# Layer 1's end: the output weights in the pool opened first, the residual rows at the head of the pool that follows

## The chip, the cores and the metric

The kernel runs on one core of a Trainium2 chip. The metric is the time of one execution on the device in microseconds; a change is judged by the medians of repeated runs of the kernel before and after it. The profile shows one execution of the kernel before, taken by the hardware profiler: the engines TensorE (PE; its weight loads PEld), VectorE (DVE), ScalarE (ACT), GpSimd (POOL) and SyncE (SP), whose queue issues the DMAs spoken of here.

## What is computed

An encoder of two layers over 2048 positions of 1024 features. Each layer is a mixer between a modulation and a normalisation with a residual:

```python
for layer in range(DEPTH):
    mod = cond @ ada_w[layer] + ada_b[layer]
    shift, scale, gate = jnp.split(mod, 3, axis=-1)
    h = x * (1.0 + scale[:, None, :]) + shift[:, None, :]
    y = even_mixer(...) if layer % 2 == 0 else odd_mixer(...)
    x = layer_norm(DEEPNORM_ALPHA * x + gate[:, None, :] * y, ln_g[layer], ln_b[layer])
```

The change lies in layer 1, whose mixer is a gated linear recurrence, run forwards and backwards over the positions:

```python
xr, g = jnp.split(h @ w_in, 2, axis=-1)
xr = centred_depthwise_conv(xr, conv_w, conv_b)
y = (rg_lru(xr, w_a[0], b_a[0], w_x[0], b_x[0], lam[0], reverse=False)
     + rg_lru(xr, w_a[1], b_a[1], w_x[1], b_x[1], lam[1], reverse=True))
return (y * jax.nn.silu(g)) @ w_out
```

## The kernel before

The positions are worked on in four tiles of C = 512 (t = 0 to 3); features lie in KD = 8 blocks of 128, called k or g. A matrix product keeps its operands as a high and a low part (hi, lo; made by `split`: ScalarE copies hi at L154, VectorE subtracts at L155) and needs three products on TensorE (`mm3`, L158 to L160): hi by hi, hi by lo, lo by hi.

Layer 1 sweeps the tiles forwards. The forward recurrence can be finished in that sweep; the backward one runs from the last position to the first, so for the tiles 0 to 2 the sweep stores what the backward one will need: for even blocks the coefficients, the inputs, the forward result and the gate (a_d, b_d, f_d, g_d), for odd blocks two arrays that need only one number per row of correction (u_d, v_d). For the last tile, t = 3, both directions are done within the sweep: `front` makes the recurrence of four blocks at a time, `back` multiplies by the gate (L1034), stores two columns to y_d (L1040), and splits the result into the operands y3 of the output product. The four blocks k = 4 to 7 come last, by `back(NT - 1, 1, f1, G1)`.

What follows the sweep:

- The output product of the last tile: `part_out` adds one block k for four groups b of 128 positions, 12 products for each half n of the 1024 output features, into the eight accumulators ps3. All 16 weight tiles (two halves by eight blocks, 512 KB each, wo_d in memory) stay in SBUF to the end: those of k = 0 to 3 in the ring of the sweep's weights (`hl`), those of k = 4 to 7 by `resident` (L1079), as tiles that are made once.
- `load_y(t)`: for t = 2, 1, 0, the operands of the output product. For an even k it loads at, bt, ft, gt (L1106, two buffers each), scans backwards on VectorE (L1113), copies one column and adds on GpSimd (L1116, L1117), multiplies by the gate on VectorE (L1118) and splits; for an odd k it loads ut and vt, corrects on VectorE (L1127) and splits. For t = 2, two columns more come from y_d (L1130).
- The residual rows z of a tile (L1151 in the kernel before, L1144 after), four of [128, 1024], from a ring of six; the sum z = ALPHA z + product on VectorE (L1166, L1179 and L1195 in the kernel before); then the normalisation: BN_STATS (L614) and an aggregate (L616) on VectorE, 1/sqrt on GpSimd (L150, L151), two steps over 1024 columns on VectorE (L623, L624), a store (L625).

Two things set the order. A scheduler orders each engine's instructions when the kernel is built, starting from the order of the text; each engine, and SyncE's queue of DMAs, then runs its own list strictly in order. And pools of SBUF are stacked from two sides: a pool that is opened after another on its side was closed takes over its memory, and each tile in it waits until whatever lay there is no longer used. Here `oq` (left) takes over from the sweep's pool `front` (closed by `sf.close()`), which held the convolution's tiles X, xc, xhi, xlo; `op` (right) takes over from `rnn` (closed by `se.close()`), which held hg, ra, T, ii, G and sg, in use until the end of `back`.

Of the kernel before, what the change touches and what calls it, by code (L numbers as in the profile page):

```python
# [7 lines left out]
F32 = mybir.dt.float32  # L8
# [10 lines left out]
KD = D // 128  # L19
C = 512  # L20
NT = S // C
# [32 lines left out]
def kernel(  # L54
# [39 lines left out]
    def pool(stack, name, side=None, bufs=1, space=None):  # L94
        kw = {} if space is None else {"space": space}
        if side is not None:
            kw["side"] = side
        return stack.enter_context(tc.tile_pool(name=name, bufs=bufs, reuse_waits="tile", **kw))
# [54 lines left out]
    def split(hi, lo, src):  # L153
        act(out=hi, in_=src, func=AF.Copy)  # L154
        tt(out=lo, in0=src, in1=hi.bitcast(F32), op=ALU.subtract)  # L155

    def mm3(ps, ahi, alo, bhi, blo, first, last):
        nc.tensor.matmul(ps, lhsT=ahi, rhs=bhi, start=first, stop=False)  # L158
        nc.tensor.matmul(ps, lhsT=ahi, rhs=blo, start=False, stop=False)  # L159
        nc.tensor.matmul(ps, lhsT=alo, rhs=bhi, start=False, stop=last)  # L160

    def bank(p, tag, shape=(128, C)):
        t = p.tile(list(shape), F32, tag=tag, name=tag)
        return t
# [353 lines left out]
    def act_pair():  # L518
        hi = cp.tile([128, 2, C], F32R, tag="act", bufs=12, name="ahi")
        lo = cp.tile([128, 2, C], F32R, tag="act", bufs=12, name="alo")  # L520
        return hi, lo
# [62 lines left out]
    def banks():  # L584
        if turn is None:
            return [bank(pj, "pj") for _ in range(4)]
        r = []
        for _ in range(4):
            r.append(bank(*((pja, "pja"), (px, "px"), (pjb, "pjb"))[turn[0] % 6 // 2]))
            turn[0] += 1  # L590
        return r
# [478 lines left out]
    def part_out(ps, hl, k):  # L1070
        for b in range(4):
            sl = slice(b * 128, b * 128 + 128)
            mm3(ps[b], y3[0][k][:, sl], y3[1][k][:, sl], hl[:, 0], hl[:, 1], k == 0, k == KD - 1)

    wo = [[None] * KD, [None] * KD]

    def resident(p, n, k):
        w = p.tile([128, 2, C], F32R, name=f"wo{n}_{k}")
        nc.sync.dma_start(out=w.bitcast(F32), in_=wo_d[n * KD + k])  # L1079
        wo[n][k] = w  # L1080

    ps3 = [banks(), [bank(pj, "pj")] + [bank(pm, "pm") for _ in range(3)]]
# [3 lines left out]
            part_out(ps3[n], wo[n][k], k)  # L1086

    oq = pool(ctx, "outq", left)
    for k in (4, 5):
        for n in range(2):  # L1090
            resident(oq, n, k)
    back(NT - 1, 1, f1, G1)
# [6 lines left out]
    def load_y(t):  # L1099
        y = ([], [])  # L1100
        n = C if t < NT - 2 else C - 2
        c0 = t * C

        def fetch(tag, src, k):
            p = oq.tile([128, C], F32, tag=tag, bufs=2, name=tag)
            load(out=p[:, 0:n], in_=src[:, k, c0:c0 + n])  # L1106
            return p

        for k in range(KD):
            if k % 2 == 0:  # L1110
                at, bt, ft, gt = (fetch(tag, src, k) for tag, src in (("at", a_d), ("bt", b_d), ("ft", f_d), ("gt", g_d)))
                h = bt[:, 0:n]
                nc.vector.tensor_tensor_scan(out=h[:, ::-1], data0=at[:, 0:n][:, ::-1], data1=h[:, ::-1],  # L1113
                                             initial=carry_b[:, t + 1, k:k + 1], op0=ALU.mult, op1=ALU.add)
                if t > 0:
                    nc.gpsimd.tensor_copy(carry_b[:, t, k:k + 1], bt[:, 0:1])  # L1116
                nc.gpsimd.tensor_tensor(out=ft[:, 0:n], in0=ft[:, 0:n], in1=h, op=ALU.add)  # L1117
                stt(out=ft[:, 0:n], in0=ft[:, 0:n], scalar=0.5, in1=gt[:, 0:n], op0=ALU.mult, op1=ALU.mult)  # L1118
                if t == NT - 2 or k < 4:
                    hi, lo = act_pair()  # L1120
                else:
                    hi, lo = (op.tile([128, 2, C], F32R, tag="act2", bufs=8, name=nm) for nm in ("ahi", "alo"))
            else:
                ft, vt = (fetch(tag, src, k // 2) for tag, src in (("ut", u_d), ("vt", v_d)))
                for u, q0, q1 in ((t, 0, C - 2), (t + 1, C - 2, C)):
                    if u < NT - 1:
                        stt(out=ft[:, q0:q1], in0=vt[:, q0:q1], scalar=cr[:, u, k // 2:k // 2 + 1],  # L1127
                            in1=ft[:, q0:q1], op0=ALU.mult, op1=ALU.add)
            if n < C:
                load(out=ft[:, n:C], in_=y_d[:, k, :])  # L1130
            split(hi[:, k % 2], lo[:, k % 2], ft)
            y[0].append(hi[:, k % 2])
            y[1].append(lo[:, k % 2])
        return y

    y2 = load_y(NT - 2)
    se.close()


    op = pool(ctx, "outp", right)  # L1140
    for k in (6, 7):
        for n in range(2):
            resident(op, n, k)
    for k in range(4, KD):  # L1144
        for n in range(2):
            part_out(ps3[n], wo[n][k], k)

    def residual_tile(t, b):
        r = t * C + b * 128
# [4 lines left out]
    zt = [residual_tile(NT - 1, b) for b in range(4)]  # L1154
    g_bc = op.tile([128, D], F32, name="g_bc1")
    b_bc = op.tile([128, D], F32, name="b_bc1")
    load(out=g_bc, in_=ln_g[1:2, :].broadcast_to([128, D]))
    load(out=b_bc, in_=ln_b[1:2, :].broadcast_to([128, D]))
    def finish(t, b, z):
# [67 lines left out]
```

## Time and profile before

| what | value |
|---|---|
| median of 3 runs (lowest, highest) | 1569.88 us (1568.82, 1575.3) |
| the profiled execution | 1567.64 us |
| its span, first to last instruction | 1565.9 us |
| busy PE, DVE, ACT, POOL | 1480.2, 1186.2, 784.1, 404.7 us |
| mean granted TensorE clock | 0.983 |

The profiled execution lies 2.2 us under the median of the runs. All moments in the text are microseconds from the span's start. A PE record of a product of 512 columns lasts 0.39 us and the next starts about 0.23 us after it, since products are pipelined; rates are therefore taken from start to start. The same holds for VectorE, where a record of 0.68 us is followed by the next after 0.60. An idle time in square brackets stands with what ended it.

### The profile page before, as it was taken

Reading aid. Unit: us, or ns where it says so; the run is one execution under the profiler, and the core shown is the slowest. Engines: PE = TensorE matmul, PEld = TensorE weight load, DVE = VectorE, ACT = ScalarE, POOL = GpSimd, SP = SyncE. Lnnn points to the kernel's source line nnn. Section 1 sums busy time; section 2 is a strip of 40 time slices with the busy share of each in tenths; the row PEclk is TensorE's granted clock in tenths of the full one; section 3 lists DMA queues with packets and bytes.
Section 4 is the critical chain, followed back from the end, with each engine's and each line's share of the span. In section 5 each row is a group of like instructions: output and inputs, shape, how many; then the busy total and the mean of one; then the engine's idle time right before and its main releaser. Section 6 shows DMA issues by size and latency. Waiting matters only on the chain. (4 is left out here: it accounts for less than half of the span.)

```text
span 1565.9 us, 22099 instructions
## 1 busy us (share of the span) xinstructions
PE 1480.2 (95%) x7096; PEld 1185.7 (76%) x7096; DVE 1186.2 (76%) x2180; ACT 784.1 (50%) x1470; POOL 404.7 (26%) x488
## 2 busy tenths in 40 slices
PE   7999999989999999999999999999999999869997
PEld 3887777657878777788887787787788788747886
DVE  4599889755859568967767775987987697788985
ACT  4677767542523332343244228499498496841100
POOL 1023233211005000300120231634644432133221
PEclk9999999999999999999999999999999999989999
DMA  9357766839788989988785699788777766369751
GB/s 348 130 170 219 224 196 189 265 120 304 243 281 298 257 255 298 314 276 262 260 296 177 195 263 275 231 259 283 224 249 271 236 226 220 111 204 340 257 193 54
DMA packets 209211, 370.91 MB, mean 237 GB/s; under 512 B 56616, under 2 KB 103620, under 8 KB 209096
## 3 DMA queue, kind: packets, MB, share of 16 engines
q1 hardware_dynamic: 202344, 354.53, 70.2%
q0 software_dynamic: 6752, 14.98, 3.7%
q8 instruction: 56, 0.92, 0.2%
q14 instruction: 59, 0.48, 0.1%
HBM read 261.96 MB, written 85.97 MB: 222 GB/s over the span
## 5 line engine op out<-in xcount | busy, mean ns | idle before, releaser
L154 ACT ACTIVATE hl<-raw 128x512 fp32r<-128x512 f32 x192 | 119.1, 628 | 227.3 <-DMA raw<-in_ev_w_in_dram 142.2
L159 PE MATMUL pj<-alo,hl 128*128 128x512 f32 x512 | 200.7, 392 | 0.0
L158 PE MATMUL pj<-ahi,hl 128*128 128x512 f32 x512 | 199.5, 392 | 1.1 <-DVE gz L753 1.1
L160 PE MATMUL pj<-ahi,hl 128*128 128x512 f32 x512 | 199.6, 391 | 0.0
L155 DVE TENSOR_TENSOR hl<-raw,hl 128x512 fp32r<-128x512 f32 x192 | 131.8, 695 | 71.5 <-ACT hl L154 70.7
L150 POOL TENSOR_SCALAR rstd<-mv 128x1 f32<-128x1 f32 x32 | 31.0, 970 | 416.5 <-DVE mv L616 305.8
L158 PEld LDWEIGHTS pj<-ahi,hl 128*128 128x128 f32 x512 | 96.5, 189 | 22.0 <-DVE gz L753 1.5
L159 PEld LDWEIGHTS pj<-alo,hl 128*128 128x128 f32 x512 | 96.6, 189 | 20.3
L160 PEld LDWEIGHTS pj<-ahi,hl 128*128 128x128 f32 x512 | 96.4, 188 | 20.2
L465 POOL DMA_DIRECT2D P<-T x112 | 62.6, 566 | 177.7 <-DVE nm L430 78.0
L158 PE MATMUL pj<-wqh,hhi 128*128 128x256 f32 (+1 forms) x256 | 88.5, 350 | 2.5 <-ACT hhi L154 1.7
L430 DVE CUSTOM_DVE_ANT_0 P<-psc,mask,nsink 128x384 f32<-128x384 f32 (+1 forms) x128 | 73.8, 593 | 22.1 <-PE psc L429 22.0
L154 ACT ACTIVATE phl<-praw 128x512 fp32r<-128x512 f32 x56 | 35.4, 631 | 105.9 <-DMA praw<-in_od_w_in_dram 51.1
L159 PE MATMUL pj<-wql,hhi 128*128 128x256 f32 (+1 forms) x256 | 88.0, 344 | 0.0
L160 PE MATMUL pj<-wqh,hlo 128*128 128x512 f32 (+1 forms) x256 | 85.7, 347 | 1.5 <-DVE hlo L155 1.5
L977 DVE SCALAR_TENSOR_TENSOR ii<-ii,xc 128x1024 f32<-128x1024 f32 (+2 forms) x32 | 40.6, 1269 | 57.6 <-ACT ii L971 57.6
L433 ACT ACTIVATE P<-P,nm 128x384 f32<-128x384 f32 (+1 forms) x128 | 76.4, 601 | 10.3 <-DVE nm L430 10.1
L777 POOL TENSOR_TENSOR alo<-hm,ahi 128x512 fp32r<-128x512 f32 x32 | 48.5, 1524 | 118.5 <-DVE hm L776 99.7
L947 DVE SCALAR_TENSOR_TENSOR xc<-X,vcol,xc 128x512 f32<-128x512 f32 (+2 forms) x96 | 75.2, 818 | 0.3
L158 PE MATMUL pm<-xhi,hg 128*128 128x512 f32 (+3 forms) x160 | 55.6, 361 | 14.1 <-ACT xhi L154 6.5
L155 DVE TENSOR_TENSOR phl<-praw,phl 128x512 fp32r<-128x512 f32 x56 | 39.1, 698 | 35.2 <-ACT phl L154 33.0
L775 ACT ACTIVATE ahi<-hm,shift,scale 128x512 fp32r<-128x512 f32 x32 | 25.2, 812 | 74.1 <-DVE hm L774 66.8
(304 smaller groups left out, 4320.1 us busy)
## 6 DMA issues: line engine op xcount, KB each, us to landing
hl<-w_d SPq DMA_DIRECT2D x128, 512.0 KB, 4.7
raw<-in_ev_w_in_dram SPq DMA_DIRECT2D x128, 256.0 KB, 4.0
w_d<-phl SPq DMA_DIRECT2D x40, 512.0 KB, 4.6
aw<-in_ada_w_dram SPq DMA_DIRECT2D x32, 512.0 KB, 6.9
hg<-w_d SPq DMA_DIRECT2D x32, 512.0 KB, 5.4
P<-T SPq DMA_DIRECT2D x104, 96.0 KB, 4.8
P<-T POOLq DMA_DIRECT2D x104, 96.0 KB, 4.2
aw<-in_ada_w_dram SPq DMA_DIRECT2D x8, 1024.0 KB, 7.7
```

What stands on the lines that cost most here:

```text
L150: nc.gpsimd.tensor_scalar(out=dst, in0=src, scalar1=mul, scalar2=EPS, op0=ALU.mult, op1=ALU.add)
L154: act(out=hi, in_=src, func=AF.Copy)
L155: tt(out=lo, in0=src, in1=hi.bitcast(F32), op=ALU.subtract)
L158: nc.tensor.matmul(ps, lhsT=ahi, rhs=bhi, start=first, stop=False)
L159: nc.tensor.matmul(ps, lhsT=ahi, rhs=blo, start=False, stop=False)
L160: nc.tensor.matmul(ps, lhsT=alo, rhs=bhi, start=False, stop=last)
L430: nc.vector.tensor_tensor_reduce(out=p[:, g, 0:W], in0=ps[:, 0:W], in1=mask[:, m0:m0 + W], scale=-0.125, scalar=nsink[:, h:h + 1], op0=ALU ...
L433: act(out=p[:, g, 0:W], in_=p[:, g, 0:W], func=AF.Exp, scale=-1.0, bias=nm[:, h:h + 1], accum_out=rs[:, h:h + 1])
L465: dma.dma_start(out=pv[32 * r:32 * r + 32, 0:nb, i], in_=T[32 * i:32 * i + 32, 0:nk].rearrange("p (j r) m -> p r j m", r=4)[:, r])
L777: nc.gpsimd.tensor_tensor(out=lo[:, j], in0=h, in1=hi[:, j].bitcast(F32), op=ALU.subtract)
L947: stt(out=xc[:, w], in0=xt[:, j0 + j:j0 + j + W], scalar=vcol1[:, 8 * j + g:8 * j + g + 1], in1=xc[:, w], op0=ALU.mult, op1=ALU.add)
L977: stt(out=ii[i][:, :, w], in0=ii[i][:, :, w], scalar=1.0, in1=xc[:, None, w].to_broadcast([128, 2, W]), op0=ALU.add, op1=ALU.mult)
```

## The change

```diff
     oq = pool(ctx, "outq", left)
-    for k in (4, 5):
+    for k in range(4, KD):
         for n in range(2):
             resident(oq, n, k)
     back(NT - 1, 1, f1, G1)
...
         def fetch(tag, src, k):
-            p = oq.tile([128, C], F32, tag=tag, bufs=2, name=tag)
+            p = op.tile([128, C], F32, tag=tag, bufs=2, name=tag)
             load(out=p[:, 0:n], in_=src[:, k, c0:c0 + n])
             return p
...
-    y2 = load_y(NT - 2)
     se.close()
     op = pool(ctx, "outp", right)
-    for k in (6, 7):
-        for n in range(2):
-            resident(op, n, k)
-    for k in range(4, KD):
-        for n in range(2):
-            part_out(ps3[n], wo[n][k], k)
...
     zt = [residual_tile(NT - 1, b) for b in range(4)]
     g_bc = op.tile([128, D], F32, name="g_bc1")
     b_bc = op.tile([128, D], F32, name="b_bc1")
+    y2 = load_y(NT - 2)
+    for k in range(4, KD):
+        for n in range(2):
+            part_out(ps3[n], wo[n][k], k)
+
     load(out=g_bc, in_=ln_g[1:2, :].broadcast_to([128, D]))
```

The weights of k = 6 and 7 move from `op` to `oq`, beside those of 4 and 5. The twelve buffers of `load_y` (24 KB of each partition) move from `oq` to `op`, so from the memory of the convolution's tiles to that of the recurrence's, behind the six residual rows and the two rows of the normalisation. In the text, the loads of the last tile's residual rows now come ahead of `load_y(2)`, and the products of k = 4 to 7 behind it.

On SyncE's queue, after the weights of k = 5 (a row is one DMA, target and source; wo_d_86 and wo_d_94 are the two halves of k = 6, wo_d_87 and wo_d_95 of k = 7):

```order
 L1079 DMA wo_5_13369<-wo_d_93 128x1024
+L1079 DMA wo_6_13371<-wo_d_86 128x1024
+L1079 DMA wo_6_13373<-wo_d_94 128x1024
+L1079 DMA wo_7_13375<-wo_d_87 128x1024
+L1079 DMA wo_7_13377<-wo_d_95 128x1024
+L1040 DMA y_d<-T 128x2 x2
+L1144 DMA z<-x_d 128x1024 x4
 L1106 DMA at<-a_d 128x510
 L1106 DMA bt<-b_d 128x510
```

The weights of k = 6, 7, the last two stores to y_d and the four residual rows now stand ahead of the first load of tile 2. Before, the same weights stood behind most of that tile's loads:

```order
 L1106 DMA gt<-g_d 128x510
-L1079 DMA wo_6_13501<-wo_d_86 128x1024
 L1106 DMA ut<-u_d 128x510
 L1130 DMA ut<-y_d 128x2
-L1079 DMA wo_6_13503<-wo_d_94 128x1024
```

On VectorE, from the last scan of the sweep on (L1113 is the scan, which these rows call by its other name; cr is the correction of the odd blocks, alo<-T the split of the last tile's k = 6 and 7), before:

```order
L1010 COPY carry_b<-T 128x1
L1113 SCALAR_TENSOR_TENSOR bt<-at,carry_b,bt 128x510
L1010 COPY carry_b<-T 128x1
L1034 SCALAR_TENSOR_TENSOR T<-T,G 128x514
L1094 COPY cr<-carry_b 128x4
```

and after, from the last of these splits on:

```order
L155 TENSOR_TENSOR alo<-T,ahi 128x512
L1164 SCALAR_TENSOR_TENSOR z<-z,pj 128x512 x2
L614 BN_STATS st_13625<-z 128x6
L1164 SCALAR_TENSOR_TENSOR z<-z,pj 128x512
L614 BN_STATS st_13636<-z 128x6
L1113 SCALAR_TENSOR_TENSOR bt<-at,carry_b,bt 128x510
L1164 SCALAR_TENSOR_TENSOR z<-z,pj 128x512 x2
L1164 SCALAR_TENSOR_TENSOR z<-z,pm 128x512 x2
L1127 SCALAR_TENSOR_TENSOR ut<-vt,cr,ut 128x510
L1164 SCALAR_TENSOR_TENSOR z<-z,pm 128x512
L614 BN_STATS st_13625<-z 128x6
L1118 SCALAR_TENSOR_TENSOR ft<-ft,gt 128x510
```

Tile 2's first scan moves from ahead of the last tile's gate product to behind three of the last tile's residual sums, and its later steps are mixed with that tile's normalisation.

On TensorE the products of tile 2 begin, in the kernel after, with the high parts of k = 0 for both halves (hl_13248 is the weight of half 0, hl_13304 of half 1; ahi_13431 and alo_13432 hold k = 0 and 1), before the low part is used:

```order
L158 MATMUL pj_13677<-hl_13248,ahi_13431 128x512
L159 MATMUL pj_13677<-hl_13248,ahi_13431 128x512
...
L158 MATMUL pm_13784<-hl_13304,ahi_13431 128x512
L159 MATMUL pm_13784<-hl_13304,ahi_13431 128x512
L160 MATMUL pj_13677<-hl_13248,alo_13432 128x512
```

Before, half 0 was worked through to k = 7 ahead of any product of half 1; now the halves are mixed up to k = 5, and the first accumulators of tile 1 are mixed with each other in the same way.

## Prediction

> **What bounds the kernel now.** I read the busy time by stretches first, then the waits of TensorE, then the chain of waits that ended last, then the timeline engine by engine. The stretches of the end of layer 1 (columns: us, busy us and instructions of PE, PEld, DVE, ACT, POOL, then granted clock, DMA share, GB/s):
>
> ```profile
> 1390.00:1400.00 10.00, 4.92 (x22) 3.75 (x20) 10.00 (x15) 1.89 (x3) 6.09 (x4) 0.94 0.63 206
> 1400.00:1410.00 10.00, 0.00 (x0) 0.00 (x0) 7.55 (x13) 1.89 (x3) 4.15 (x4) 0.50 0.84 239
> 1410.00:1420.00 10.00, 7.18 (x25) 5.77 (x26) 5.57 (x8) 2.42 (x4) 2.45 (x2) 0.70 1.01 382
> ...
> 1425.50:1469.40 43.90, 43.90 (x193) 36.01 (x192) 40.87 (x56) 5.69 (x9) 16.21 (x17) 1.00 0.92 333
> 1469.40:1513.40 44.00, 44.00 (x193) 36.04 (x192) 43.90 (x64) 4.41 (x7) 14.67 (x16) 1.00 0.51 169
> 1513.40:1557.40 44.00, 44.00 (x193) 35.88 (x192) 23.38 (x30) 0.00 (x0) 8.00 (x10) 1.00 0.24 84
> ```
>
> After 1425.5 TensorE never rests: three token tiles (I call them y2, y1, y0 after the code) of 192 products take 43.9 to 44.0 us each, 0.229 us a product. The one hole is ahead of it. In y2 and y1 VectorE is nearly full as well (40.87 of 43.90, 43.90 of 44.00), which decides below how far TensorE can be brought forward. The waits of TensorE in this end of the program, the chain, and the products at the borders:
>
> ```profile
> PE pj L158 <- DMA wo<-wo_d: 17.9, 1, 17.9
> ```
> ```profile
> 1380.85 6.44 DMA at<-a_d
> ...
> 1393.42 1.19 DVE bt L1113
> ...
> 1406.06 6.62 DMA wo<-wo_d
> 1412.82 0.77 PE pj L158
> ...
> 1557.44 0.24 PE pm L160
> ```
> ```profile
> 1394.54 0.39 PE L160 MATMUL pm<-wo,alo 128*128 128x512 f32 x1
> 1412.82 0.77 PE L158 MATMUL pj<-wo,ahi 128*128 128x512 f32 x1 [17.89 <-DMA wo<-wo_d]
> 1425.52 0.39 PE L158 MATMUL pj<-hl,ahi 128*128 128x512 f32 x1
> 1469.42 0.39 PE L158 MATMUL pj<-hl,ahi 128*128 128x512 f32 x1
> ```
>
> The last tile's products for k = 6 and 7 wait 17.9 us for output weights. The load was issued only at 1406.06, and the queue shows why:
>
> ```profile
> 1378.61 2.19 SPq L1079 DMA_DIRECT2D wo<-wo_d  x4
> 1380.85 0.44 SPq L1106 DMA_DIRECT2D at<-a_d  x1
> ...
> 1387.31 0.32 SPq L1106 DMA_DIRECT2D at<-a_d  x1
> 1387.98 0.32 SPq L1106 DMA_DIRECT2D bt<-b_d  x1
> ...
> 1390.75 0.32 SPq L1106 DMA_DIRECT2D vt<-v_d  x1
> ...
> 1396.08 0.99 SPq L1040 DMA_DIRECT2D y_d<-T  x2
> ...
> 1406.06 0.42 SPq L1079 DMA_DIRECT2D wo<-wo_d  x1
> ```
>
> SyncE issues in order; the weights of k = 6, 7 stand behind loads of y2 that wait for buffers. From 1394.77 (the last start of k = 5 plus 0.23) to 1425.52 are 30.75 us, in which 48 products need 48 x 0.229 = 11.0. So 19.8 us are lost: 18.05 of idling, and 1.7 because the 48 products took 12.7 us (the first record lasts 0.77, not 0.39).
>
> **The change, part by part.** *The weights go ahead of y2's loads.* All eight are now issued from 1378.61; four took 2.19 us to issue, so eight end at about 1383. They no longer bound k = 6. What is late next is the data of k = 6, the step T<-T,G (L1034):
>
> ```profile
> 1393.61 1.90 POOL L1017 TENSOR_TENSOR T<-T 128x514 f32<-128x514 f32 x1 [1.32 <-DVE carry_b L1010]
> ```
> ```profile
> 1394.58 1.48 DVE L1034 SCALAR_TENSOR_TENSOR T<-T,G 128x514 f32<-128x514 f32 x1
> 1396.05 0.68 DVE L1034 SCALAR_TENSOR_TENSOR T<-T,G 128x514 f32<-128x514 f32 x1
> ```
>
> The scan of y2 (1.19 us in the chain) no longer stands ahead of it, so it starts there, at 1393.4, and, slowed by the add of 1393.61 as the row of 1394.58 was, ends at 1395.0; ScalarE's half of the split is 0.63 us (row below), and products can start at 1395.9, 1.1 us after k = 5. At full clock they end at 1395.9 + 11.0 = 1406.9.
>
> *Y2's loads come later and behind four residual rows.* They now sit in the memory of T, ra and ii. The queue has the two y_d stores first, which wait for the second L1034 (about 1396.1), then four residual loads of 512 KB, then at, bt, ft, gt. Before, four weight loads of the same size led them: from the first issue at 1378.61, at had landed 8.7 us later (1380.85 + 6.44), bt some 0.7 after that, and vt was issued into its next buffer turn 12.1 us after. With the residual rows issued from 1396.8, at lands at 1405.5, bt at 1406.2 and vt at 1408.9. What used to be hidden behind TensorE's 1380 to 1395 is now in the open; that is the price of the change.
>
> *VectorE's order.* Between the last split of the last tile and y2's first scan stand three residual sums (L1164) and two BN_STATS. They wait for TensorE's k = 7, whose third bank ends after 33 products at 1403.5, so the landing of bt, not they, sets the scan. The durations from there:
>
> ```profile
> 1410.17 0.63 ACT L154 ACTIVATE ahi<-ft 128x512 fp32r<-128x512 f32 x1 [4.07 <-DVE ft L1118]
> ```
> ```profile
> 1398.47 0.68 DVE L1118 SCALAR_TENSOR_TENSOR ft<-ft,gt 128x510 f32<-128x510 f32 x1
> 1399.07 0.68 DVE L155 TENSOR_TENSOR alo<-T,ahi 128x512 fp32r<-128x512 f32 x1
> ...
> 1433.10 2.46 DVE L624 SCALAR_TENSOR_TENSOR z<-z,rstd,b_bc 128x1024 f32<-128x1024 f32 x2
> ```
> ```profile
> L1117 POOL TENSOR_TENSOR ft<-ft,bt 128x512 f32<-128x512 f32 (+1 forms) x6 | 8.7, 1454 | 10.4 <-DMA ft<-f_d 7.7 <-ACT ahi L154 2.6
> ...
> L1116 POOL COPY carry_b<-bt 128x1 f32<-128x1 f32 x5 | 2.5, 502 | 18.8 <-DVE bt L1113 18.8
> ```
>
> A step of 512 columns costs 0.6 us (start to start), one of 1024 and a scan 1.2. Scan of k = 0: 1406.2 to 1407.4. Four residual sums, the ut step, one sum and one BN_STATS (7 x 0.6 = 4.2), 0.9 for GpSimd in the way (next paragraph), then ft<-ft,gt (0.6): 1413.1. GpSimd's add (0.5 and 1.45 us after the scan, 1409.4) is hidden behind that. ScalarE 0.63: 1413.7, and the first product of y2 at 1414.0. Gap: 1414.0 - 1406.9 = 7.1 us.
>
> *The clock.* After such a gap it falls, as the 17.9 us did; even 3.2 us did it:
>
> ```profile
> 1367.47 0.39 PE L158 MATMUL pm<-xhi,hg 128*128 128x258 f32 x1 [3.21 <-ACT ra L966]
> ```
> ```profile
> 1369.00:1370.00 1.00, 1.00 (x6) 0.82 (x5) 1.00 (x2) 0.86 (x3) 0.00 (x0) 0.50 0.00 0
> ```
>
> I take the same 1.7 us again; the bounds are 0 (a gap much under 3 us) and twice 1.7.
>
> *GpSimd against VectorE.* Two overlapping rows:
>
> ```profile
> 1482.76 2.32 DVE L1113 TENSOR_TENSOR_SCAN bt<-at,carry_b,bt 128x512 f32<-128x512 f32 x1
> ```
> ```profile
> 1482.39 1.61 POOL L1117 TENSOR_TENSOR ft<-ft,bt 128x512 f32<-128x512 f32 x1 [4.50 <-DVE bt L1113]
> ```
>
> The scan took 1.1 us more than its 1.2 and ended 1.1 after the add. L1034 at 1394.58 lost 0.8 in the same way, the one at 1396.05 nothing. I take 0.9 for each of the 12 adds of y2, y1 and y0 (bounds 0 and 1.45). The Trainium skill (SBUF — State Buffer, section Who interferes with whom) says that a GpSimd operation and a VectorE operation with two SBUF inputs take an exclusive lock, and the later one blocks until the first is done. The row of 1482.76 agrees; by that rule alone each add would cost up to its whole 1.45 us.
>
> *Does y2 keep fed?* TensorE's new order does k = 0 of both halves with the high parts first, and mixes the halves so that 116 products come ahead of the first of k = 6. VectorE's list from the scan at 1406.2 to the last split of y2 holds 5 scans, 8 steps of 1024 columns, 6 BN_STATS, 5 sums, 8 combining steps (ut, ft), 8 splits and 4 aggregates (0.5 in all): 13 x 1.2 + 27 x 0.6 + 0.5 = 32.3, with 4 x 0.9 in all 35.9, so 1442.1. TensorE wants k = 6 at 1414.0 + 1.7 + 116 x 0.229 = 1442.3. Just in time; I put 0.6 for small waits. Y2 ends at 1414.0 + 43.9 + 1.7 + 0.6 = 1460.2 instead of 1469.4.
>
> *And y1, y0?* VectorE's last splits of y2, y1 and y0 before, with the scan that begins most of y0's work:
>
> ```profile
> 1418.21 0.69 DVE L155 TENSOR_TENSOR alo<-ft,ahi 128x512 fp32r<-128x512 f32 x1
> ...
> 1463.12 0.69 DVE L155 TENSOR_TENSOR alo<-ft,ahi 128x512 fp32r<-128x512 f32 x1
> 1463.73 1.28 DVE L1113 TENSOR_TENSOR_SCAN bt<-at,carry_b,bt 128x512 f32<-128x512 f32 x1
> ...
> 1499.65 0.67 DVE L155 TENSOR_TENSOR alo<-ft,ahi 128x512 fp32r<-128x512 f32 x1
> ```
>
> By the same count y1's list (5 scans, 29 steps of 512, small ones 1.3) is 24.7 + 3.6 = 28.3 us, to 1470.4, and y0's (2 scans, 9 steps of 1024, 30 of 512, small ones 1.1) 32.3 + 3.6 = 35.9, to 1506.3. TensorE, ahead by 9, wants y1's k = 6 low part after 57 products, at 1473.3, and y0's after 20 of its own, at 1460.2 + 44.0 + 4.6 = 1508.8. Both are met, by 2 to 3 us. Before, y0 was ready at 1500.3 and wanted at 1469.4 + 44.0 + 4.6 = 1518.0; the change spends most of that reserve.
>
> **Sum.** Lost before 19.8. Lost after: 1.1 + 7.1 + 1.7 + 0.6 = 10.5. Gain 9.3 us; the tail behind the last product (1557.44 to the span's end at 1565.9) stays. The profiled execution took 1567.64 us, so 1558.3 in its terms; it lies 2.2 under the median of the three runs, 1569.88, from which the forecast is 1560.5. About 0.5% (7.9 us) is what a measurement of this kernel can tell from no change.
>
> **Rivals.** *The feed is quicker* (loads land 2 us sooner than counted, no cold clock worth naming): y2 starts at 1411, loses 4.1 + 1.1, gain 14.6, 1555.3. For it: nothing else is in flight when the residual rows start; against: the chain's own 6.44 us for at behind four such loads.
>
> *VectorE gives the gain back.* If each add blocks for its whole length, 12 x 0.55 = 6.6 us more stand on VectorE by y0, against 2.5 of reserve: TensorE waits 4.1, gain 5.2, 1564.7; with stores in the queue that wait for L624 ahead of y2's last loads, a few us more. For it: the stretches' 40.87 and 43.90. Against: not every overlap costs, the second L1034 ran its 0.68 beside GpSimd's next work. The rule of the Trainium skill quoted above (SBUF — State Buffer) would make this case the likely one.
>
> *Slower: VectorE becomes the bound to the end.* From 1406.2 twelve pairs of k must be made, and 172 products (39.3 us) follow the last: the end is unchanged at 9.3 us a pair, 0.5% slower from 10.0. My count is (1506.3 - 1406.2) / 12 = 8.3. If each pair is made serially, load, scan, add, split, as y2's four were before without norm work ((1418.9 - 1393.4) / 4 = 6.4, to the end of its last split), with 4.9 of norm work on top, a pair takes 11.3 and the end is 24 us later: 1594. Against: y0's pairs, with norm work between, took (1500.3 - 1463.7) / 4 = 9.1.
>
> *It does not do what it says:* the weights' memory is still in use and they land as late as before. The order has them behind the same waits as k = 4, 5, whose loads were issued at once: little for it; 1569.9.
>
> **Chances.** Forecast 0.50 (own range 1558 to 1562.5), quicker feed 0.17, given back 0.26, slower 0.04, nothing 0.03. Of the forecast's 0.50 some 0.04 lies past 1562.0: faster 0.63, same 0.33, slower 0.04. The range leaves out a little of each end: 1555 to 1567.5.
>
> **What would show it.** In the new profile: no wait of TensorE on wo; products of k = 6 at about 1396; a gap of about 7 us ended by ahi of y2, with clock 0.5 behind it; y2's scan held by bt, not by the residual sums; no gap over 1 us in y1 and y0. Gaps of several us there, or a scan later than 1409, make it wrong; so does a gap under 4 us.

## The result, and the profile after

The kernel after takes 1563.14 us in the median of 8 runs (1553.9 to 1572.19), the kernel before, in 8 runs with the three of the table above among them, 1570.78. The ratio estimated from these runs is 0.9936 with a 95% interval of 0.9913 to 0.996: 0.64% faster, about 10 us, and 6 to 14 by the interval. The two medians differ by 7.6 us. The forecast from the earlier median was 1560.5, in a range of 1555 to 1567.5. The profiled execution took 1562.55 us, its span is 1560.8.

In this execution the sweep's end lies 3.4 us later than in that of before, from parts of the program that the change does not touch (TensorE's wait at 1367.47 before stands at 1370.86 here): its last scan (L1007) starts at 1394.70 instead of 1391.32. So this section and the experiments use one stretch, from the start of that scan to the start of the last product:

| | last scan of the sweep | last product | stretch |
|---|---|---|---|
| before | 1391.32 | 1557.28 | 165.96 |
| after | 1394.70 | 1552.18 | 157.48 |

The stretch became 8.5 us shorter; the forecast had 9.3. With the 19.8 us that were lost before, a stretch without any loss would be 146.2 us, so 11.3 are lost now. The waits of TensorE at this end of the program:

```profile
PE pj L158 <- ACT ahi L154: 8.2, 1, 8.2
...
PE pj L160 <- DVE alo L155: 0.6, 2, 0.3
```

The 17.9 us on wo are gone. In their place stands one wait of 8.2 us on ahi. TensorE's products at the borders (last of k = 5, first of k = 6, last of k = 7, first of y2, first of y1):

```profile
1397.88 0.39 PE L160 MATMUL pm<-wo,alo 128*128 128x512 f32 x1
1398.27 0.50 PE L158 MATMUL pj<-wo,ahi 128*128 128x512 f32 x1
...
1409.46 0.39 PE L160 MATMUL pm<-wo,alo 128*128 128x512 f32 x1
1418.03 0.80 PE L158 MATMUL pj<-hl,ahi 128*128 128x512 f32 x1 [8.17 <-ACT ahi L154]
...
1464.33 0.39 PE L158 MATMUL pj<-hl,ahi 128*128 128x512 f32 x1
```

Products follow each other by 0.23 us from start to start. K = 6 waits 0.2 us; k = 6 and 7 take 11.4 instead of 11.0 (1398.27 to 1409.69); the gap is 8.3; y2 takes 46.3 instead of 43.9. That is 0.2 + 0.4 + 8.3 + 2.4 = 11.3, so y1 and y0 lose nothing. By stretches (the gap, y2, y1, y0; columns as before):

```profile
1410.00:1418.00 8.00, 0.00 (x0) 0.00 (x0) 6.80 (x11) 1.26 (x2) 1.44 (x2) 0.64 0.93 294
1418.00:1464.30 46.30, 45.98 (x192) 37.60 (x193) 43.37 (x55) 6.96 (x11) 21.06 (x20) 0.95 0.97 340
1464.30:1508.30 44.00, 43.74 (x192) 35.67 (x191) 44.00 (x64) 6.96 (x11) 15.92 (x16) 1.00 0.67 218
1508.30:1552.30 44.00, 44.00 (x195) 36.16 (x193) 32.68 (x43) 0.00 (x0) 9.47 (x13) 1.00 0.30 111
```

VectorE was busy for 23.38 us of y0 before and is now for 32.68: its work has not grown, TensorE has come closer to it. SyncE's queue shows the eight weights in a row, and y2's first loads behind the stores and the residual rows:

```profile
1381.99 4.56 SPq L1079 DMA_DIRECT2D wo<-wo_d  x8
1397.58 2.30 SPq L1040 DMA_DIRECT2D y_d<-T  x2
1399.94 1.94 SPq L1144 DMA_DIRECT2D z<-x_d  x4
1402.05 0.32 SPq L1106 DMA_DIRECT2D at<-a_d  x1
```

VectorE in the gap, then GpSimd's add and ScalarE's half of the split of k = 0:

```profile
1411.20 1.28 DVE L1113 TENSOR_TENSOR_SCAN bt<-at,carry_b,bt 128x510 f32<-128x510 f32 x1 [1.46 <-DMA bt<-b_d]
1412.40 1.26 DVE L1164 SCALAR_TENSOR_TENSOR z<-z,pj 128x512 f32<-128x512 f32 x2
1413.58 1.28 DVE L1164 SCALAR_TENSOR_TENSOR z<-z,pm 128x512 f32<-128x512 f32 x2
1414.77 0.75 DVE L1127 SCALAR_TENSOR_TENSOR ut<-vt,cr,ut 128x510 f32<-128x510 f32 x1
1415.43 0.68 DVE L1164 SCALAR_TENSOR_TENSOR z<-z,pm 128x512 f32<-128x512 f32 x1
1416.03 0.69 DVE L614 BATCH_NORM_STATS2 st<-z 128x6 f32<-128x512 f32 x1
1416.63 0.68 DVE L1118 SCALAR_TENSOR_TENSOR ft<-ft,gt 128x510 f32<-128x510 f32 x1
```
```profile
1412.72 1.27 POOL L1117 TENSOR_TENSOR ft<-ft,bt 128x510 f32<-128x510 f32 x1
```
```profile
1417.34 0.63 ACT L154 ACTIVATE ahi<-ft 128x512 fp32r<-128x512 f32 x1 [1.16 <-DVE ft L1118]
```

The scan waits for bt until 1411.20. GpSimd has done its add at 1413.99, and then ft<-ft,gt still stands 2.6 us in VectorE's list, behind residual sums, the ut step and a BN_STATS. The gap has two halves: the loads, then the place in VectorE's list.

The chain of waits that ended last comes into y1 by its loads and VectorE; before, it came by the output weights:

```profile
1468.45 3.69 DMA bt<-b_d
...
1477.17 0.57 DVE alo L155
1477.78 0.50 PE pj L160
```

TensorE waited only 0.26 us there, yet the chain passes: y1's last split ended when it was wanted, and no reserve was left.

### The profile page after: what moved, and what is told of

Read it like the earlier page. It is cut to its first block, busy times and chain, and to the rows that moved or that the text cites. A ratio compares the mean times of both kernels' runs of the same rounds, so it can differ in the third digit from the quotient of the medians.

```text
span 1560.8 us, 22092 instructions
## 1 busy us (share of the span) xinstructions
PE 1481.5 (95%) x7096; PEld 1185.4 (76%) x7096; DVE 1188.0 (76%) x2180; ACT 783.5 (50%) x1470; POOL 405.1 (26%) x488
## 5 line engine op out<-in xcount | busy, mean ns | idle before, releaser
L150 POOL TENSOR_SCALAR rstd<-mv 128x1 f32<-128x1 f32 x32 | 27.4, 857 | 401.6 <-DVE mv L616 289.9
L433 ACT ACTIVATE P<-P,nm 128x384 f32<-128x384 f32 (+1 forms) x128 | 76.4, 601 | 11.6 <-DVE nm L430 11.4
```

The lines of the kernel that those rows point to most:

```text
L150: nc.gpsimd.tensor_scalar(out=dst, in0=src, scalar1=mul, scalar2=EPS, op0=ALU.mult, op1=ALU.add)
L433: act(out=p[:, g, 0:W], in_=p[:, g, 0:W], func=AF.Exp, scale=-1.0, bias=nm[:, h:h + 1], accum_out=rs[:, h:h + 1])
```

## The experiments

The theory: the change takes the wait on the weights away and uncovers y2's first loads, whose landing, with VectorE's steps behind it, is the new gap; from y2 on, VectorE's supply has almost no reserve. The rivals: the landing alone sets everything, or VectorE alone does. Each edit is against the kernel after unless said otherwise. "Gap" is TensorE's longest idle time between the last product of k = 5 and y2's first.

| kernel | stretch | gap | median of its runs | ratio to before (95%) |
|---|---|---|---|---|
| before | 165.96 | 17.9, for wo | 1570.78 | – |
| after | 157.48 | 8.2 | 1563.14 | 0.9936 (0.9913 to 0.996) |
| e1 residual rows late | 165.36 | 17.7 | 1569.49 | 0.9991 (0.9968 to 1.0015) |
| e2 two more rows | 161.93 | 9.8 | 1565.84 | 0.9966 (0.9942 to 0.999) |
| e3 filler | 157.10 | 0.5 | 1560.22 | 0.9938 (0.9914 to 0.9961) |
| e4 first pair early | 150.35 | none | 1560.24 | 0.9922 (0.9891 to 0.9953) |
| e5 no GpSimd add | 152.59 | 4.6 | 1556.24 | 0.9902 (0.9888 to 0.9915) |
| e6 the same, filler | 151.87 | none | 1553.56 | 0.9886 (0.9871 to 0.99) |
| e7 rows by ScalarE | 154.46 | 5.5 | 1561.69 | 0.9937 (0.9917 to 0.9956) |
| e8 two steps early | 153.51 | 0.8 | 1557.92 | 0.9906 (0.989 to 0.9923) |
| e9 add on VectorE | 158.19 | 10.1 | 1562.37 | 0.9951 (0.9931 to 0.9971) |
| e10 e4 and e9 | 149.86 | none | 1553.2 | 0.9881 (0.9839 to 0.9923) |
| e11 e4, e7 and e9 | 151.12 | 0.8 | 1554.65 | 0.9903 (0.9867 to 0.9939) |
| e12 text order only | 163.29 | 14.1, for wo | 1569.29 | 0.9987 (0.9965 to 1.0008) |

Each ratio is to runs of the kernel before from the same set, whose medians are 1570.58 (e1 to e4), 1571.81 (e5 to e8) and 1569.23 (e9 to e12).

Times of one kernel spread over up to 21 us (the kernel before in one set of 29: 1562.06 to 1582.68). The stretch leaves out what varies ahead of it: the rest of the span took between 1397.8 and 1407.6 us in the fourteen profiled executions. Verdicts on mechanisms therefore go by the stretch of one profiled execution of each kernel. In the kernel after, e3, e5, e6 and e9, whose queues are alike up to y2's first scan, this scan starts 15.95 to 16.50 us behind the sweep's last scan; so differences of less than about 1 us between stretches are not read. Most intervals of the ratios overlap with that of the kernel after, so its time alone ranks few of the experiments.

**e1, the weights alone.** The residual rows go behind y2 in the text.

```diff
+    y2 = load_y(NT - 2)
     zt = [residual_tile(NT - 1, b) for b in range(4)]
...
-    y2 = load_y(NT - 2)
```

> The change without its second half: all weights of k = 4 to 7 lie in the early pool and are loaded first, but the four residual rows of the last tile are issued behind all of y2's loads. Theory (the residual rows free the PSUM banks that y2 needs, so they have to land before y2's first product, whatever at and bt do): the rows wait behind buffer turns of y2's third and fourth pair, are issued at about 10 us behind the first load of y2, and land some 5 us later; VectorE's first residual sum then comes 15 us or more behind the first load, y2's first scan about 5 us behind it. The gap ahead of y2 is ended by a residual sum, not by ahi, and is 11 to 13 us where the changed kernel has 8.2; the time is 3 to 5 us above the changed kernel's. Rival (only the landing of at and bt sets the gap, the sums have time): y2's first scan comes 5 us sooner, the gap is 3 to 4 us and the time 4 us below the changed kernel's.

The stretch is 165.36: nothing of the gain is left. SyncE's queue, and the first product of y2:

```profile
1403.53 0.42 SPq L1106 DMA_DIRECT2D at<-a_d  x1
...
1422.21 1.94 SPq L1144 DMA_DIRECT2D z<-x_d  x4
```
```profile
1431.11 0.77 PE L158 MATMUL pj<-hl,ahi 128*128 128x512 f32 x1 [17.66 <-DVE z L1164]
```

The rows were issued 18.7 us behind at, since buffer turns of all four pairs stood ahead of them. TensorE waited 17.7 us for a residual sum, longer than expected (11 to 13), though the split of y2's k = 0 was done by 1413.4. Two things held the sum until 1430.28: no row had landed before 1429.5 (7.3 us behind its issue at least), and VectorE's list has the first sum behind the last of y2's splits, which it follows at once. The theory holds against its rival: the rows free the accumulators, so they belong ahead. In this order the weights' part of the change is worth nothing without the rows' part.

**e2, more ahead of y2's loads.**

```diff
     zt = [residual_tile(NT - 1, b) for b in range(4)]
+    zn = [residual_tile(NT - 2, b) for b in range(2)]
...
-    zt = [residual_tile(NT - 2, b) for b in range(4)]
+    zt = zn + [residual_tile(NT - 2, b) for b in range(2, 4)]
```

> The changed kernel with two more residual rows (512 KB each, of the next tile, needed later anyway) issued between the four and y2's loads. Theory (at and bt land in the order of issue behind everything that is ahead of them, and their landing holds the scan that ends the gap): 1 MB more at the 319 GB/s of that stretch is 3.3 us, so the scan of y2's k = 0 starts 3.3 us later and the gap is 11.5 instead of 8.2 us; the time is about 3 us above the changed kernel's. Rival (VectorE's residual sums, which stand between scan and ft<-ft,gt, set the end of the gap): with more of them done before the scan, the gap grows by less than 1 us and the time stays.

```profile
1415.74 1.28 DVE L1113 TENSOR_TENSOR_SCAN bt<-at,carry_b,bt 128x510 f32<-128x510 f32 x1 [0.77 <-DMA bt<-b_d]
```

The scan comes 18.9 us after the sweep's last scan (1396.88 here) instead of 16.5, so 1 MB ahead costs about 2.4 us of landing (3.3 expected). The gap grew by only 1.6, because VectorE did seven residual sums before the scan instead of three: the rival has part of it. The stretch is 4.4 us longer all the same; the rest, 2.8 us, are three waits inside y1:

```profile
1471.95 0.51 PE L158 MATMUL pj<-wo,ahi 128*128 128x512 f32 x1 [1.19 <-ACT ahi L154]
1474.91 0.50 PE L160 MATMUL pj<-wo,alo 128*128 128x512 f32 x1 [1.07 <-DVE alo L155]
1481.68 0.50 PE L160 MATMUL pj<-wo,alo 128*128 128x512 f32 x1 [0.52 <-DVE alo L155]
```

When y2's feed comes later, y1's comes too late.

**e3, the price of the slow clock.** TensorE works through the gap on products whose result is thrown away.

```diff
+        if n == 0:
+            for i in range(32):
+                nc.tensor.matmul(ps[0], lhsT=wo[0][0][:, 0, 0:128], rhs=wo[0][0][:, 1], start=True, stop=True)
         for k in range(KD):
```

> The changed kernel with 32 more products of 128 x 512 (7.3 us at full clock) on resident weights ahead of y2's first product, written into the bank that y2's first product then starts anew. TensorE works through the gap. Theory (the gap costs 2.0 us of slow clock beyond itself): the granted clock stays 1.0, y2's 192 products take 44.3 us instead of 46.3, and the time is 2 us below the changed kernel's. Rival (y2 is held to VectorE's pace anyway): TensorE waits for alo or ahi in y2 by what the clock gave, y1's first product comes at the same time as without the filler, and the time stays. If the filler outlasts the gap, y2 starts later by up to 1 us.

Y2's first product and y1's, a stretch over y2, and one of the first us of y2 in the kernel after (granted clock third from the end):

```profile
1421.82 0.50 PE L158 MATMUL pj<-hl,ahi 128*128 128x512 f32 x1 [0.53 <-ACT ahi L154]
...
1466.78 0.39 PE L158 MATMUL pj<-hl,ahi 128*128 128x512 f32 x1
```
```profile
1421.80:1468.20 46.40, 45.68 (x199) 37.18 (x200) 43.95 (x56) 6.97 (x11) 20.91 (x21) 1.00 0.98 341
```
```profile
1420.00:1421.00 1.00, 1.00 (x4) 0.81 (x3) 1.00 (x3) 0.56 (x1) 1.00 (x1) 0.50 0.96 295
```

At clock 1.00 y2 takes 45.0 us instead of 46.3. Inside it TensorE waited 0.7 us for alo, and 0.3 in the kernel after; without these waits the difference is 1.7. Yet the stretch is only 0.4 shorter, which is not read as a difference. The gain was given back in y0:

```profile
1516.88 0.50 PE L160 MATMUL pj<-wo,alo 128*128 128x512 f32 x1 [1.61 <-DVE alo L155]
```

So the slow clock costs about 1.7 us, and whoever removes it alone gains nothing: VectorE's last split of y0 bounds the end from there. The rival was right about the outcome, with the wait in y0 and not in y2.

**e4, y2's k = 0 under cover again.** One of the two buffers of at, bt, ft and gt lies in the early pool, behind the weights; the memory of both pools together is the same.

```diff
-            p = op.tile([128, C], F32, tag=tag, bufs=2, name=tag)
+            q, m = (oq, 1) if tag in ('at', 'bt', 'ft', 'gt') and k % 4 == 0 else (op, 1) if tag in ('at', 'bt', 'ft', 'gt') else (op, 2)
+            p = q.tile([128, C], F32, tag=tag, bufs=m, name=tag)
```

> The changed kernel with one of the two buffers of at, bt, ft and gt in the early pool (memory in all as before), so that y2's k = 0 loads stand behind the weights and ahead of the residual rows, in the shadow of TensorE's last products of k = 0 to 5. Theory (the gap is the price of y2's first loads, which lost their cover): the scan of k = 0 is done at the time of L1034, TensorE can do the 24 products of k = 0 (5.5 us) as soon as residual sums free banks; the wait before them is 2 us or less, a second one before k = 1 is about 3 us; with 1.2 us more before k = 6 the time from the last k = 5 product to y1's first falls from 66.5 to 61 to 63 us and the time by 3 to 5 us. Rival (VectorE's supply is the bound from y2 on): the first gap shrinks, but waits of the same sum appear inside y2 and y1; the time is within 1 us of the changed kernel's.

```profile
1386.27 0.46 SPq L1107 DMA_DIRECT2D at<-a_d  x1
```
```profile
1400.87 1.27 DVE L1114 TENSOR_TENSOR_SCAN bt<-at,carry_b,bt 128x510 f32<-128x510 f32 x1
1403.73 0.69 DVE L1119 SCALAR_TENSOR_TENSOR ft<-ft,gt 128x510 f32<-128x510 f32 x1 [1.58 <-POOL ft L1118]
```
```profile
1409.74 0.39 PE L158 MATMUL pj<-hl,ahi 128*128 128x512 f32 x1
1411.91 0.50 PE L158 MATMUL pj<-hl,ahi 128*128 128x512 f32 x1 [0.65 <-DVE z L1165]
...
1424.54 0.50 PE L158 MATMUL pj<-hl,ahi 128*128 128x512 f32 x1 [1.97 <-ACT ahi L154]
```

at is issued at 1386.27 instead of behind the rows, and y2's first product follows the last of k = 7 without a gap. The stretch falls by 7.1 us, more than the 3 to 5 expected: the clock stays at 1.00, the scan landed behind L1034 and cost k = 6 nothing, and no wait appeared in y1 or y0, since VectorE had k = 0 behind it. The gap was the price of loads without cover. E4 takes away both halves of it at once, since ft<-ft,gt now stands ahead of all residual sums. The median of e4's six runs lies only 2.9 us under the kernel after's, with overlapping intervals. The same edit on top of e9 (e10, below) is clearer: 8.3 us of the stretch and 9.2 of the median, within one set of runs.

**e5 and e6, without GpSimd's additions.** L1117 is left out (ft + bt is not computed); e6 also has 20 of the filling products of e3.

```diff
-                nc.gpsimd.tensor_tensor(out=ft[:, 0:n], in0=ft[:, 0:n], in1=h, op=ALU.add)
```

> The changed kernel without the 12 additions on GpSimd (L1117) in y2, y1 and y0; ft + bt is left out of the computation, all else stays. Measure: the stretch from the start of the sweep's last scan (L1007) to the last product of the kernel, 166.0 us before and 157.5 in the changed kernel. Theory (each add costs VectorE up to 0.9 us and stands between scan and ft<-ft,gt; VectorE's supply is what y2 waits for behind the gap): scans take 1.2 to 1.3 us throughout, the gap ahead of y2 is about 5.5 us instead of 8.2, no wait on alo is left, and the stretch is 154 to 155 us. Rival (the landing of at and bt alone holds the end, the adds lie beside other work): the gap is over 7 us and the stretch 156.5 to 157.5.

> The same without GpSimd's adds, and with 20 filling products (4.6 us) on TensorE in the gap. With VectorE lightened the clock should show its price: theory (the slow clock after the gap costs 2.0 us, hidden with the adds in because y2 then waits for VectorE's alo): the stretch is 1.5 to 2 us shorter than in the run without adds and without filler, 152 to 153.5 us. Rival (the slow clock costs nothing, its work is caught up): the same stretch as there.

VectorE's groups over the 118 us from the sweep's last scan, in the kernel after and in e5 (count, then busy us and mean ns of one):

```profile
L1127 DVE SCALAR_TENSOR_TENSOR ut<-vt,cr,ut 128x510 f32<-128x510 f32 (+1 forms) x20 | 15.6, 809 | 0.1
L155 DVE TENSOR_TENSOR alo<-ut,ahi 128x512 fp32r<-128x512 f32 x12 | 9.1, 758 | 0.0
L155 DVE TENSOR_TENSOR alo<-ft,ahi 128x512 fp32r<-128x512 f32 x12 | 9.0, 750 | 0.1
```
```profile
L1126 DVE SCALAR_TENSOR_TENSOR ut<-vt,cr,ut 128x510 f32<-128x510 f32 (+1 forms) x20 | 9.9, 523 | 1.0 <-DMA ut<-u_d 1.0
L155 DVE TENSOR_TENSOR alo<-ft,ahi 128x512 fp32r<-128x512 f32 x12 | 8.1, 678 | 0.8 <-ACT ahi L154 0.8
L155 DVE TENSOR_TENSOR alo<-ut,ahi 128x512 fp32r<-128x512 f32 x12 | 8.1, 675 | 0.0
```

These three groups cost 7.6 us more beside the additions, 0.63 for each of the 12 (0.9 was forecast); with L624, where 8 steps took 1392 ns each instead of 1267, it is 0.72. The stretch is 152.59, below what was expected: of the 4.9 us gained, 3.6 are the gap, and 3.05 of these lie between the scan and the first product (3.8 us here, 6.8 in the kernel after), since ft<-ft,gt stands behind two residual sums instead of seven steps. In e6 the stretch is 0.7 us shorter still (1.5 to 2 expected), less than a difference that is read here, and TensorE waited 0.8 for alo; so the price of the clock rests on e3.

**e7, the rows on another queue.**

```diff
-        load(out=z, in_=x1_d[r:r + 128, :])
+        (nc.scalar.dma_start if t == NT - 1 else load)(out=z, in_=x1_d[r:r + 128, :])
```

> The changed kernel with the four residual rows of the last tile issued by ScalarE, so that at and bt of y2 lead SyncE's queue. Theory (at and bt land late because they stand behind 2 MB in one queue): beside the rows, on shared engines, at and bt land 3 us sooner at least, the gap ahead of y2 falls from 8.2 to 5 to 6 us, unless the rows, now up to 1.5 us later, hold it; the stretch from L1007 to the last product is 154.5 to 156 us. Rival (the 16 engines' rate is the limit and what is in flight shares it, so that the queue makes no difference): at and bt land with the rows, the gap is 7.5 us or more and the stretch 157 to 158.

```profile
1409.23 1.28 DVE L1113 TENSOR_TENSOR_SCAN bt<-at,carry_b,bt 128x510 f32<-128x510 f32 x1 [8.93 <-DMA gt<-g_d]
```

The stretch is 154.46, at the short end of what the theory had, but not for its reason. The scan comes 15.15 us behind the sweep's last scan (1394.08 here) instead of 16.50, 1.35 us sooner and not 3, and at was issued 0.65 sooner. The rest of the gain of 2.65 in the gap is the place of ft<-ft,gt, 4.2 us behind the start of the scan instead of 5.4. The queue as such made 0.7 us at most, and perhaps nothing: in e3, e5, e6 and e9 the same scan stands at 15.95 to 16.12. Nor did at and bt lead: ScalarE issued the rows from 1398.95 on, 1.8 us ahead of at, which had the y_d stores before it. So e7 does not test loads that lead the rows; e4 does, for k = 0. The Trainium skill (DMA: Bandwidth & Descriptors, section Queues, rings and completion order) has queues share the same engines, served in turn by packets; that the data came so little sooner agrees with it.

**e8, k = 1 ahead of the rows too,** on top of e4:

```diff
+            if t == NT - 2 and k == 2:
+                zt.extend(residual_tile(NT - 1, b) for b in range(4))
...
-    zt = [residual_tile(NT - 1, b) for b in range(4)]
+    zt = []
```

> The kernel with y2's k = 0 in the early pool (stretch 150.4 us), with the residual rows moved behind the loads of k = 1 too (0.5 MB, 1.5 us). Theory (what is left there is the wait of 2.0 us for k = 1, which is a matter of when its loads land): that wait goes, the rows and with them the sums that free the banks come up to 1.5 us later; the stretch is 149 to 150.5 us. Rival (k = 1 waits for VectorE's residual sums ahead of its step, not for its loads): k = 1 gains nothing, the sums come later, and the stretch is 151 to 153.

The stretch is 153.51, 3.2 us longer than e4 and a little past the rival's 151 to 153, by its mechanism: the first residual sum came at 1410.69, held by its row, and behind k = 1 TensorE waited 2.96 us for ahi, with 1.15 more in y0.

**e9, the additions on VectorE.**

```diff
-                nc.gpsimd.tensor_tensor(out=ft[:, 0:n], in0=ft[:, 0:n], in1=h, op=ALU.add)
+                tt(out=ft[:, 0:n], in0=ft[:, 0:n], in1=h, op=ALU.add)
```

> The changed kernel with the 12 additions ft + bt on VectorE instead of GpSimd. Theory (beside GpSimd each add cost VectorE 0.72 us, by the run without adds, and 1.5 us of way in the chain of each k; on VectorE it costs 0.6 and no way): a gap of about 5.3 us and a stretch from the last scan of the sweep to the last product of 154 to 155.5 us, 157.5 in the changed kernel. Rival (VectorE, full from 1415 to 1520 in the changed kernel, becomes the bound with 7.2 us more of its own): waits on alo or ahi of over 1 us in y2, y1 or y0, and a stretch of 157 to 160 us.

```profile
1410.86 1.28 DVE L1113 TENSOR_TENSOR_SCAN bt<-at,carry_b,bt 128x510 f32<-128x510 f32 x1 [1.45 <-DMA gt<-g_d]
...
1418.66 0.67 DVE L1118 SCALAR_TENSOR_TENSOR ft<-ft,gt 128x510 f32<-128x510 f32 x1
```

My expectation failed: the gap is 10.1, not 5.3. The scheduler's new list puts the add behind three residual sums and ft<-ft,gt 7.8 us behind the scan's start, where e5 had 2.4. The stretch lies in the rival's range, but its waits did not come: none of TensorE is left in y2, y1 and y0. Behind the gap the exchange pays some 1.2 us (the gap is 1.9 longer, the stretch only 0.7), little more than is read here.

**e10 and e11, combinations.** The edits of e4 and e9, then with that of e7.

> Y2's k = 0 in the early pool and the additions on VectorE, together. Theory (the two gains have different places: the loads' cover, and VectorE's pace): the stretch is 148 to 150 us, 150.4 with the first alone. Rival (with k = 0 early TensorE is at VectorE's heels, and 7 us more of VectorE's own work show as waits): 150.5 to 153 us.

> The same two, and the last tile's residual rows issued by ScalarE. Theory (with the rows out of SyncE's queue, k = 1 of y2 lands some 3 us sooner, as k = 0 did in the changed kernel with that edit): the wait before k = 1 goes and the stretch is 147.5 to 149.5 us. Rival (the rows share the rate, land later, and free the banks later, which is what TensorE waits for first here): 150 to 152 us.

e10 has 149.86, within what was expected and within 1 us of e4; with k = 0 early there is no gap whose end VectorE's order could set, and four waits of about 1 us or less are left in y2:

```profile
PE pj L158 <- ACT ahi L154: 2.0, 2, 1.0
PE pj L158 <- DVE z L1165: 0.6, 2, 0.4
```

e11 has 151.12: the rows land later beside the loads and the sums that free the banks hold TensorE three times, 2.4 us in all, as its rival had it; the wait for ahi that was to go is still 1.8 us. The best version that computes everything is e10, 1553.2 us, a ratio of 0.9881 (0.9839 to 0.9923) to the kernel before; the intervals of e4 and e11 overlap with it.

**e12, from the kernel before: only the place of the weights of k = 6, 7 in the text.**

```diff
-    y2 = load_y(NT - 2)
     se.close()
     op = pool(ctx, "outp", right)
     for k in (6, 7):
         for n in range(2):
             resident(op, n, k)
+    y2 = load_y(NT - 2)
```

> The kernel before with one edit: the weights of k = 6, 7 stand ahead of y2's loads in the text, but still in the pool that follows the sweep. Theory (their memory, not their place in the text, holds the loads: it comes free at the sweep's end, behind the sweep's stores and three rounds of y2's buffers): they are issued at most 2 us sooner than before, and the stretch is 163 to 166 us against 166.0. Rival (the place in the text would have been enough): they are issued right behind those of k = 4, 5, y2's loads keep their cover, and the stretch is 147 to 150 us.

```profile
1402.89 1.86 SPq L1079 DMA_DIRECT2D wo<-wo_d  x4
```

The stretch is 163.29, and TensorE still waits 14.1 us for wo: the text is not enough. The weights, whose memory comes free at the sweep's end, were still issued behind loads of three pairs of y2, 13.8 us behind the sweep's last scan (1389.10 here), 14.7 before.

## Why the prediction was right, and where its sizes were off

- *The weights.* Right: issued in a row from 1381.99, no wait on wo. The wait ahead of k = 6 was 0.2 us, not 1.1: I had let GpSimd's add slow the first L1034 (1.48 in the profile of before); here it ran its 0.68, with the add begun 0.12 us after it. The copy L1094 behind it took 1.07 us instead of 0.16. The second L1034 behind that lost 0.3 at most, since it needs the result of the same add, which was done at 1398.51. From there the way leads to the rows: L1034 ends at 1399.54, its store to y_d is issued at 1399.56, the rows from 1399.94.
- *The landing of y2's loads, the term most off.* The residual rows were issued 5.2 us behind the sweep's last scan, as forecast (1396.8 - 1391.3 = 5.5). But bt was there 11.3 us after that (1399.94 to 1411.20), not 9.4. The queue was of the same make in the profile of before: four loads of 512 KB, then at, bt, ft and gt. The rate was the same too: in the 8.7 us from the first issue, 2.68 MB were moved here and 2.69 before. But before, at had landed by then, 6.4 us behind its issue; here it took 8.3, and 3.32 MB had been moved, of which the rows and at are 2.36. So loads from behind it were served ahead of its last piece. Why more of them here than before stays open; no run separates it. E3, e5, e6 and e9 repeat it, with a scan 10.7 to 10.9 us behind the first row.
- *Scan to first product.* 6.8 us against 7.8, so the gap is 8.3 against 7.1. The count of steps in VectorE's list was the right model: the seven took 4.2. The 0.9 for GpSimd in the way was not paid here, since the add lay beside residual sums. The list's length was read off the order and has a price of its own, which I did not see as one: the bare way from scan to ft<-ft,gt is 2.9 us (e4), the list makes it 5.4.
- *The clock.* Forecast 1.7; e3 measures about 1.7. With 0.6 for small waits, y2 was to lose 2.3, and lost 2.4, though its waits were only 0.3. The Trainium skill (TensorE: Matmul & The Clock Gate, section Part 1: The HAM clock gate) gives about 3.4 us of steady work until the full clock is back; here the clock stood at 0.50 from 1418 to past 1422, some 4 us.
- *GpSimd against VectorE.* 0.63 us an add on the three groups shown, against 0.9 and the bound of 1.45. The price falls on steps that read two arrays from SBUF (and on one copy, shown at the end); the residual sums, which read PSUM, kept their 0.60 beside the add of 1412.72. The Trainium skill's rule (SBUF — State Buffer, section Who interferes with whom) names the former, and the trace agrees in this; the blocked time was not the whole add, because part of the adds lay beside sums.
- *Y1 and y0.* No gap over 1 us, as forecast. The reserve of 2 to 3 us was not there: y1's last split came at 1477.10 and was waited for by 0.26, y0's, below, ended at 1511.8 where 1512.9 was wanted. Shifted by the 3.4 us, y1's is 4 us and y0's 2 us later than counted. E2 and e3 show what follows: 1 to 2 us more on either side and TensorE waits in y1 or y0. So the rival in which VectorE gives the gain back was one step away.

```profile
1511.13 0.67 DVE L155 TENSOR_TENSOR alo<-ft,ahi 128x512 fp32r<-128x512 f32 x1
```

The gain of the stretch, 8.5 us, is the forecast's 9.3 + 0.9 (k = 6) - 1.2 (gap) - 0.5 (k = 6 and 7, y2). The mechanism came as forecast: no wait on wo, a gap ended by ahi with the scan held by bt, and no gap in y1 and y0. The scan, at 1407.8 on the clock of the profile of before, kept the 1409 that was set for it. That the sum came so close is in part luck: the late landing (1.6 us) was largely offset by a term for GpSimd that was not paid and by k = 6.

## What to carry to other kernels

Before you move loads to the head of a queue, look for what was hidden behind the stall that goes, and keep one step of that under cover (here 8 KB of each partition for k = 0, worth 7 us of the stretch). The stall was also the reserve of the next supplier, so count that reserve down to the last tile. Where a scheduler orders an engine, read in the new order where the step stands that ends the gap, and price that place by itself.

## What was not expected of the hardware

- One MB more in the queue moved the scan behind it by 2.4 us. The rows' 2 MB on a second queue, still issued first, moved it by 0.7 at most beyond what at's earlier issue explains.
- A VectorE copy of 4 columns took 1.07 us beside a GpSimd add of 1396.99 to 1398.51 and ended at 1398.54, with it: this short step too was held to the add's end. In the profile of before, begun at 1395.98 between two adds, it took 0.16.

```profile
1397.47 1.07 DVE L1094 COPY cr<-carry_b 128x4 f32<-128x4 f32 x1
```
```profile
1396.99 1.52 POOL L1017 TENSOR_TENSOR T<-T 128x514 f32<-128x514 f32 x1 [1.31 <-DVE carry_b L1010]
```

- The clock that a filler keeps up was worth 1.7 us in y2 and nothing that can be read at the end of the program.
